# Gate matrices of a PEER layer: accumulated in DRAM by indirect transfers instead of one-hot matmuls

## The chip, the cores and the metric

The kernel runs on one core of a Trainium2 chip. The metric is the device time of one execution in microseconds (us); smaller is better. TensorE appears as PE (its weight loads as PEld), VectorE as DVE, ScalarE as ACT, GpSimd as POOL and SyncE as SP. Each of them executes its own list of instructions strictly in order.

## The reference

One layer of a residual block for 1024 tokens of width 1024, in float32. A mixer (mLSTM heads and gMLP groups, then an output projection) is followed by PEER, a layer of 16384 single-neuron experts. Per token and head (8 heads), two top-16 searches over 128 keys each give 256 candidate sums, of which the 16 best name 16 experts:

```python
s1, i1 = lax.top_k(s[:, :, 0], PEER_TOPK)
s2, i2 = lax.top_k(s[:, :, 1], PEER_TOPK)
cand = s1[..., :, None] + s2[..., None, :]          # reshaped to 256
cand_idx = i1[..., :, None] * PEER_KEYS + i2[..., None, :]
top_s, pos = lax.top_k(cand, PEER_TOPK)
idx = jnp.take_along_axis(cand_idx, pos, axis=-1)
gate = jax.nn.softmax(top_s, axis=-1)
...
a = jax.nn.gelu(jnp.einsum('td,thkd->thk', xb, ub))  # ub, vb: rows idx of expert_u, expert_v
out = jnp.einsum('thk,thkd->td', a * gb, vb)
```

So each token has 8 x 16 = 128 pairs of an expert (i, j), each index below 128, and a gate. Written as a matrix, the gates of a token are G[j, i], zero but for those pairs; where two heads of a token pick the same expert, their gates add up.

## The kernel before, in words

The tokens are eight blocks of 128. Blocks 0 to 4 are "dense": for them every expert is computed by matmul and multiplied with the gate matrix. Blocks 5 to 7 are "sparse": their experts' rows are gathered from DRAM by indirect transfers that POOL issues, and DVE does the dot products and sums.

**The front** goes over three parts, `PARTS = [(0, 2), (2, 3), (5, 3)]`: blocks 0 and 1, blocks 2 to 4, blocks 5 to 7. In each part come the normalisation (`scales`, ending in the reciprocal root `rx`), the mixer's steps (`head`, `group`), the output projection, a second normalisation (`rall`, one per block, made on POOL by `rstd` and needed by the transposes ahead of the queries), and the eight query heads, whose scores go to DRAM (`d_sc`). Between the query heads run the top-16 searches of the part's first block (`topk_units`; `merge16` does four heads at a time, so each block has two merges).

**Side work.** While part p+1 runs, the gate matrices of part p's dense blocks and the remaining top-16 searches are interleaved with it (`side_units`, `interleave`): blocks 0 and 1 beside part 1, blocks 2, 3 and 4 beside part 2. A gate matrix is made four tokens at a time (`gate_units`): DVE writes one-hots AB of both indices by comparing with `iota`, ACT scales one of them by the gates, PE multiplies them into PSUM tile pG (4 matmuls), ACT copies pG into Gt, and after 32 tokens ACT issues the store of Gt (2 MB) to `d_G`.

**The dense phase** (`experts`) has 32 groups of four expert rows i. Stage 1 reads the group's gates from `d_G` into tile Gin (one buffer), computes x times u (tile pa), gelu, times Gin (DVE), and splits the product into wh and wl. Stage 2 multiplies with v (tile pout) and DVE adds it to the accumulator. POOL makes the low halves ulo and vlo and issues the sparse blocks' gathers (768 of them, 128 rows of 4 KB each).

**What sets the order.** The program is written in the order above; a scheduler of the tile layer then fixes each engine's list at build time by its own estimates. On the chip nothing is moved any more: an instruction waits for its semaphores, and all behind it on its engine wait too. POOL's list holds the small steps of both normalisations and of the mixer (`rstd` at lines 62 and 63 of before, 61 and 62 of the change; the products `vv` at 409 and 410), so whatever stands ahead of them delays them.

Of the kernel before, what the change touches and what calls it, by code (L numbers as in the profile page):

```python
# [22 lines left out]
NEXP = 128  # L23
EPS = 1e-6
KAPPA = 0.25 * 128.0 ** -0.5
TG = 32
# [3 lines left out]
GS = 4  # L30
HB = 4
MMB = 2
TPB = 2
# [13 lines left out]
class Build:  # L47
# [124 lines left out]
    def consts(self, cp):  # L172
# [9 lines left out]
        self.rall = cp.tile([128, 8], F32, name="rall", tag="rall")  # L182
        self.mhalf = cp.tile([128, 16], F32, name="mhalf", tag="mhalf")
# [269 lines left out]
    def topk_units(self, blk):  # L453
# [15 lines left out]
        def merge(h0):  # L469
            ijg = st["ijg"]  # L470
            self.merge16(h0, st["tv"], st["ti"], ijg)
            if blk in self.sparse:
# [4 lines left out]
                hl = slice(h0 * 16, (h0 + HB) * 16)  # L477
                v.scalar_tensor_tensor(ix[:, hl], ijg[:, 0, hl], float(NEXP), ijg[:, 1, hl], op0=OP.mult, op1=OP.add)
                v.tensor_copy(gt[:, hl], ijg[:, 2, hl])

        def done():
            ijg = st["ijg"]
            if blk in self.dense:
                pt = self.gps.tile([128, 3, 128], F32, name="pG", tag="pG", bufs=2)
                for k in range(3):
                    nc.tensor.transpose(pt[:, k], ijg[:, k], self.ident)
                t = self.gp.tile([128, 3, 128], F32, name="ijgT", tag="ijgT", bufs=1)
                nc.scalar.activation(t, pt, AF.Copy)
                self.pick[blk] = t
# [5 lines left out]
        return L + [done]  # L495
# [145 lines left out]

    def gate_units(self, blk):
        nc = self.nc
        pool = self.gp
        s = self.dense.index(blk)
        st = {}

        def quad(tt, q):
            t3 = self.pick[blk]
            if q == 0:  # L650
                st["G"] = pool.tile([128, NEXP, TG], F32, name="Gt", tag="Gt", bufs=2)
            Gt = st["G"]
            pg = self.gps.tile([128, 4, 128], F32, name="pG", tag="pG", bufs=2)
            AB = pool.tile([128, 2, 4, 128], F32, name="AB", tag="AB", bufs=NAB)
            t0 = tt * TG + q * 4
# [7 lines left out]
            if q == TG // 4 - 1:  # L663
                nc.scalar.dma_start(self.d_G[s * (128 // TG) + tt], Gt)

        return [lambda tt=tt, q=q: quad(tt, q) for tt in range(128 // TG) for q in range(TG // 4)]

# [88 lines left out]
    def experts(self, side, dp, ps):  # L756
# [6 lines left out]
        T2 = T // 2  # L763
        n32 = T // TG
        ngroups = NEXP // GS
        W, V, st = {}, {}, {"n": 0}

        def stage1(g, e):
            if e == 0:
                st["G"] = dp.tile([128, n32, GS, TG], F32, name="Gin", tag="Gin", bufs=1)  # L770
                nc.sync.dma_start(st["G"], self.d_G[:, :, g * GS:(g + 1) * GS].rearrange("n j i t -> j n i t"))
# [10 lines left out]
            for s in range(2):  # L782
                pa = ps.tile([128, T2], F32, name="pa", tag="pa", bufs=3)
# [9 lines left out]
        def stage2(g):  # L793
# [9 lines left out]
            for s in range(ND):  # L803
                for d in range(2):
                    if st["n"] % 3 == 0:
                        po = ps.tile([128, 512], F32, name="pout", tag="pout", bufs=1)
                    else:
                        po = self.gps.tile([128, 512], F32, name="pout", tag="pG", bufs=2)
# [188 lines left out]
```

## Time and profile before

| | us |
|---|---|
| median of three runs | 2876.03 (2875.09 to 2885.14) |
| the profiled execution's own time | 2879.65 |
| span of that execution | 2877.8 |
| PE busy | 2708.7 (94%) |
| DVE busy | 2195.1 (76%) |
| POOL busy | 1501.2 (52%) |
| ACT busy | 1120.9 (39%) |

The span is the time from the first instruction to the last; the rest of the execution's time lies around it. The front lasts until about 992 us after the span's start, the dense phase from there to the end. POOL's busy time does not count register and semaphore instructions.

### The profile page before, as it was taken

The page shows a single profiled execution, that of the slowest core. Times are in us where ns is not written, and L with a number is a line of the kernel's source. Part 1 is how long each engine was busy: PE and PEld are TensorE (multiplying, and loading weights), DVE is VectorE, ACT ScalarE, POOL GpSimd, SP SyncE. Part 2 cuts the span into 40 slices and gives each one's busy share as a digit, 9 for nine tenths or more (in the row PEclk, how much of TensorE's full clock was granted, in tenths as well). Part 3 has the DMA queues.
Part 4 walks back from the last instruction along what each step waited for, and adds up shares of the span by engine and source line. Part 5 has one row for each costly group of instructions (what it writes and reads, how often), then busy time and mean ns, then how long its engine had stood idle before and what let it go on. Part 6 is the DMA issues. An engine that isn't in the chain of part 4 may idle for free.

```text
span 2877.8 us, 44768 instructions
## 1 busy us (share of the span) xinstructions
PE 2708.7 (94%) x16283; PEld 2470.3 (86%) x16283; DVE 2195.1 (76%) x4981; ACT 1120.9 (39%) x2295; POOL 1501.2 (52%) x1220
## 2 busy tenths in 40 slices
PE   7888989999898799999989999999999999999998
PEld 7887989889898798888878889889888899888987
DVE  6649975289985677888887787978987777777774
ACT  5444788348888332223222222223222232222222
POOL 3430010000100186777766677767767777768772
PEclk9989999999999899999999999999999999999999
DMA  7798557866578798998988999998889999989992
GB/s 245 256 313 281 188 211 280 276 223 225 187 272 302 264 326 300 323 336 306 333 288 304 336 321 331 308 342 308 309 280 331 344 327 332 334 314 332 326 345 95
DMA packets 327821, 838.41 MB, mean 291 GB/s; under 512 B 25520, under 2 KB 161072, under 8 KB 315824
## 3 DMA queue, kind: packets, MB, share of 16 engines
q0 software_dynamic: 114048, 427.87, 40.2%
q1 hardware_dynamic: 190544, 347.91, 37.5%
q10 hardware_dynamic: 23008, 59.77, 5.3%
q8 instruction: 128, 2.10, 0.3%
q14 instruction: 93, 0.76, 0.1%
HBM read 746.32 MB, written 89.13 MB: 290 GB/s over the span
## 4 chain that ended last, share of the span: by engine, by line
PE 58%; DVE 17%; DMA 9%; issue 6%; ACT 4%; POOL 4%; SPq 1%; ACTq 1%; POOLq 0%; DVEq 0%
PE pa L96 7%; PE pa L94 7%; PE pa L95 7%; PE pout L94 7%; PE pout L95 7%; PE pout L96 7%; DMA Gin<-d_G 3%; PE pG L661 3%; DVE sacc L713 2%; DVE gat L697 2%; PE pq L94 2%; PE pq L96 1%; PE pq L95 1%; DVE AB L656 1%; DMA raw<-v 1%
## 5 line engine op out<-in xcount | busy, mean ns | idle before, releaser
L94 PE MATMUL pa<-xh,uhi 128*128 128x320 f32 x2048 | 639.7, 312 | 42.2 <-DVE wl L790 26.4
L95 PE MATMUL pa<-xl,uhi 128*128 128x320 f32 x2048 | 637.3, 311 | 0.0
L96 PE MATMUL pa<-xh,ulo 128*128 128x320 f32 x2048 | 626.3, 312 | 4.2 <-POOL ulo L779 3.9
L94 PE MATMUL pout<-vhi,wh 128*128 128x512 f32 x1280 | 503.5, 398 | 17.4 <-DVE acc L814 15.4
L713 DVE SCALAR_TENSOR_TENSOR sacc<-gat,aw,sacc 128x1024 f32<-128x1024 f32 x384 | 492.3, 1282 | 30.6 <-DMA gat<-v,ix 22.8
L95 PE MATMUL pout<-vlo,wh 128*128 128x512 f32 x1280 | 507.4, 398 | 0.0
L709 POOL DMA_INDIRECT gat<-v,ix x384 | 364.3, 949 | 240.7 <-DVE sacc L713 140.0
L96 PE MATMUL pout<-vhi,wl 128*128 128x512 f32 x1280 | 488.5, 398 | 0.0
L693 POOL DMA_INDIRECT gat<-u,ix x384 | 365.5, 952 | 202.6 <-DVE gat L697 102.3
L697 DVE SCALAR_TENSOR_TENSOR gat<-gat,xn 128x1024 f32<-128x1024 f32 x384 | 459.5, 1212 | 15.3 <-DMA gat<-u,ix 15.1
L94 PEld LDWEIGHTS pa<-xh,uhi 128*128 128x128 f32 x2048 | 389.6, 190 | 56.1 <-DVE wl L790 30.7
L96 PEld LDWEIGHTS pa<-xh,ulo 128*128 128x128 f32 x2048 | 386.1, 190 | 11.1 <-POOL ulo L779 7.1
L95 PEld LDWEIGHTS pa<-xl,uhi 128*128 128x128 f32 x2048 | 389.6, 190 | 6.9
L779 POOL TENSOR_TENSOR ulo<-raw,uhi 128x1024 fp32r<-128x1024 f32 x128 | 309.0, 2416 | 144.0 <-ACT uhi L778 142.1
L800 ACT ACTIVATE vhi<-raw 128x1024 fp32r<-128x1024 f32 x128 | 131.8, 1052 | 504.4 <-PE pout L95 442.3
L801 POOL TENSOR_TENSOR vlo<-raw,vhi 128x1024 fp32r<-128x1024 f32 x128 | 307.9, 2416 | 34.1 <-ACT vhi L800 31.7
L94 PEld LDWEIGHTS pout<-vhi,wh 128*128 128x128 f32 x1280 | 241.7, 189 | 73.7 <-DVE acc L814 19.2
L814 DVE TENSOR_TENSOR acc<-acc,pout 128x512 f32<-128x512 f32 x320 | 214.5, 682 | 109.1 <-PE pout L96 96.0
L95 PEld LDWEIGHTS pout<-vlo,wh 128*128 128x128 f32 x1280 | 242.2, 189 | 50.6 <-POOL vlo L801 0.4
L96 PEld LDWEIGHTS pout<-vhi,wl 128*128 128x128 f32 x1280 | 240.2, 189 | 52.8
L788 DVE TENSOR_TENSOR pa<-pa,Gin 128x320 f32<-128x320 f32 x256 | 126.6, 494 | 202.2 <-ACT pa L786 108.0
L789 ACT ACTIVATE wh<-pa 128x320 fp32r<-128x320 f32 x256 | 111.8, 437 | 423.7 <-DVE pa L788 340.7
(243 smaller groups left out, 5039.4 us busy)
## 6 DMA issues: line engine op xcount, KB each, us to landing
raw<-uT SPq DMA_DIRECT2D x128, 512.0 KB
raw<-v SPq DMA_DIRECT2D x128, 512.0 KB
wlo<-d_wl SPq DMA_DIRECT2D x48, 1024.0 KB
d_G<-Gt ACTq DMA_DIRECT2D x20, 2048.0 KB
Gin<-d_G SPq DMA_DIRECT2D x32, 1280.0 KB
wraw<-win SPq DMA_DIRECT2D x72, 512.0 KB
d_wl<-wlo POOLq DMA_DIRECT2D x24, 1024.0 KB
wraw<-wq SPq DMA_DIRECT2D x48, 512.0 KB
```

The lines of the kernel that those rows point to most:

```text
L94: te.matmul(ps, lh, rh, start=k == 0, stop=False)
L95: te.matmul(ps, lh, rl, start=False, stop=False)
L96: te.matmul(ps, ll, rh, start=False, stop=k == n - 1)
L693: gd = nc.gpsimd.indirect_dma_start(out=t, out_offset=None, in_=self.I["u"], in_offset=bass.IndirectOffsetOnAxis(ap=st["ix"][:, k:k + 1], ...
L697: v.scalar_tensor_tensor(t, t, 1.0, st["xn"], op0=OP.mult, op1=OP.mult, accum_out=st["a"][:, k:k + 1])
L709: gd = nc.gpsimd.indirect_dma_start(out=t, out_offset=None, in_=self.I["v"], in_offset=bass.IndirectOffsetOnAxis(ap=st["ix"][:, k:k + 1], ...
L713: v.scalar_tensor_tensor(st["acc"], t, st["a"][:, k:k + 1], st["acc"], op0=OP.mult, op1=OP.add)
L779: nc.gpsimd.tensor_tensor(ul, ur, uh.bitcast(F32), op=OP.subtract)
L788: v.tensor_tensor(p3, p3, G[:, s * (n32 // 2):(s + 1) * (n32 // 2), e], op=OP.mult)
L800: nc.scalar.activation(vh, vr, AF.Copy)
L801: nc.gpsimd.tensor_tensor(vl, vr, vh.bitcast(F32), op=OP.subtract)
L814: v.tensor_add(st["acc"][:, s, dl], st["acc"][:, s, dl], po)
```

## The change

The gate matrices no longer come from one-hots and matmuls. There is now one DRAM tensor per dense block, laid out as [j, i, token]. SP stores zeros into it (4 transfers of 2 MB per block). Then POOL issues, for each of the 128 (head, rank) pairs of a block, one indirect transfer with accumulation: 128 single floats, one per token, each added at its own address. DVE computes the addresses (`dix`) from the indices and the token number (`pcol`). The transfers of one head (16 of them) may overlap; those of the next head of the same block wait until all 16 of the head before have landed, since two heads of a token may name the same expert. That makes 5 x 128 = 640 indirect transfers and 20 clearing stores; gone are the one-hots, their matmuls, the two PSUM banks of pG and the 20 stores of Gt. The two banks go to the front's tiles (3 buffers each in place of 2) and to pout. A group's gates are read by five transfers with rows of 2 KB instead of one with rows of 512 bytes, and stage 1 takes the 640 tokens in pieces of 256 and 384 in place of 320 and 320.

```diff
-MMB = 2
-TPB = 2
+MMB = 3
+TPB = 3
...
-        def done():
...
-                pt = self.gps.tile([128, 3, 128], F32, name="pG", tag="pG", bufs=2)
...
+                at = tk.tile([128, 16 * HB], F32, name="at", tag="at", bufs=1)
+                v.tensor_scalar(at, ijg[:, 0, hl], 128.0, self.pcol, op0=OP.mult, op1=OP.add)
+                v.scalar_tensor_tensor(ix[:, hl], ijg[:, 1, hl], 128.0 * NEXP, at, op0=OP.mult, op1=OP.add)
+            v.tensor_copy(gt[:, hl], ijg[:, 2, hl])
...
+    def clear_units(self, blk):
+
+        s = self.dense.index(blk)
+        self.cleared[blk] = []
+        flat = self.d_G[s].rearrange("j i t -> j (i t)")
+
+        def clear(q):
+            out = flat[:, q * 4096:(q + 1) * 4096].rearrange("j (a c) -> j a c", c=1024)
+            d = self.nc.sync.dma_start(out, self.zero[:, None, :].to_broadcast([128, 4, 1024]))
+            self.tc.keep_in_program_order(d)
+            self.cleared[blk].append(d.ins)
+
+        return [lambda q=q: clear(q) for q in range(4)]
+
     def gate_units(self, blk):
...
-            nc.vector.tensor_tensor(AB, self.iota[:, None, None, :].to_broadcast([128, 2, 4, 128]),
-                                    t3[:, 0:2, t0:t0 + 4, None].to_broadcast([128, 2, 4, 128]), op=OP.is_equal)
-            for u in range(4):
-                nc.scalar.activation(AB[:, 1, u], AB[:, 1, u], AF.Copy, scale=t3[:, 2, t0 + u:t0 + u + 1])
-            for u in range(4):
-                nc.tensor.matmul(pg[:, u], AB[:, 1, u], AB[:, 0, u], start=True, stop=True)
-            nc.scalar.activation(Gt[:, :, q * 4:q * 4 + 4], pg.rearrange("p q i -> p i q"), AF.Copy)
...
+        def some(h, q):
+            ix, gt = self.pick[blk]
+            key = f"G{blk}h{h}"
+            for k in range(h * 16 + q * 4, h * 16 + q * 4 + 4):
+                d = nc.gpsimd.indirect_dma_start(out=flat, out_offset=bass.IndirectOffsetOnAxis(ap=ix[:, k:k + 1], axis=0),
+                                                 in_=gt[:, k:k + 1], in_offset=None, compute_op=OP.add).ins
+                tc.declare_no_dep(d, group=key, reason="the experts of one head of a token differ, tokens differ")
+                tc.add_to_no_dep_group(key, d)
+                for e in st["before"]:
+                    tc.add_manual_dep(d, e.name, sync, reason="after the head before")
+                st["now"].append(d)
+            if q == 3:
+                st["before"], st["now"] = st["now"], []
+                self.filled[blk] = st["before"]
+
+        return [lambda h=h, q=q: some(h, q) for h in range(8) for q in range(4)]
...
-        T2 = T // 2
+        halves = [(0, ND // 2), (ND // 2, ND)]
...
-                nc.sync.dma_start(st["G"], self.d_G[:, :, g * GS:(g + 1) * GS].rearrange("n j i t -> j n i t"))
+                st["G"] = dp.tile([128, ND, GS, 128], F32, name="Gin", tag="Gin", bufs=1)
+                for b, blk in enumerate(self.dense):
+                    d = nc.sync.dma_start(st["G"][:, b], self.d_G[b][:, g * GS:(g + 1) * GS])
+                    for f in self.filled[blk]:
+                        self.tc.add_manual_dep(d.ins, f.name, sync, reason="after the last head")
...
+                    po = ps.tile([128, 512], F32, name="pout", tag="pout", bufs=3)
```

What this does to POOL's list is seen at two places. The first is the end of the mixer in part 1 (the norm `rall` of blocks 2 to 4 is what the queries of that part wait for; d_G_63 is the gate tensor of block 1, and x16 stands for 16 transfers in a row). Before:

```order
L63 TENSOR_TENSOR grr<-grr,mhalf 128x3
L409 TENSOR_TENSOR vv<-vv,lng 128x384
L410 TENSOR_TENSOR vv<-vv,lnb 128x384
L392 MEMSET ws 64x64
L62 TENSOR_SCALAR rall<-ss 128x1
```

Now:

```order
L62 TENSOR_TENSOR grr<-grr,mhalf 128x3
L672 DMA d_G_63<-dgt,dix 2097152x1 x15
L414 TENSOR_TENSOR vv<-vv,lng 128x384
L672 DMA d_G_63<-dgt,dix 2097152x1
L397 MEMSET ws 64x64
L415 TENSOR_TENSOR vv<-vv,lnb 128x384
L672 DMA d_G_63<-dgt,dix 2097152x1 x16
L397 MEMSET ws 64x64
L672 DMA d_G_63<-dgt,dix 2097152x1 x16
L61 TENSOR_SCALAR rall<-ss 128x1 x2
```

Where the steps of the mixer stood next to each other, transfers of block 1 now stand between them, and 32 more stand right ahead of `rall`. From the last store of part 0's weights to this `rall` POOL's list now holds 240 of the 640 transfers; 80 more stand from there to the first step of part 2's mixer (64 of these behind `rx`), 272 more up to `rall` of part 2.

The second place is the end of part 2 on the same engine, where the front gives way to the dense phase (d_G_66 is block 4; ulo is the dense phase's first step on POOL). Before:

```order
L62 TENSOR_SCALAR grr<-mv 128x3
L63 TENSOR_TENSOR grr<-grr,mhalf 128x3
L409 TENSOR_TENSOR vv<-vv,lng 128x384
L410 TENSOR_TENSOR vv<-vv,lnb 128x384
L62 TENSOR_SCALAR rall<-ss 128x1
L63 TENSOR_TENSOR rall<-rall,mhalf 128x1
...
L779 TENSOR_TENSOR ulo<-raw,uhi 128x1024 x2
```

Now:

```order
L415 TENSOR_TENSOR vv<-vv,lnb 128x384
L672 DMA d_G_66<-dgt,dix 2097152x1 x32
L61 TENSOR_SCALAR rall<-ss 128x1 x2
L62 TENSOR_TENSOR rall<-rall,mhalf 128x1 x2
L61 TENSOR_SCALAR rall<-ss 128x1
L62 TENSOR_TENSOR rall<-rall,mhalf 128x1
L672 DMA d_G_66<-dgt,dix 2097152x1 x48
L799 TENSOR_TENSOR ulo<-raw,uhi 128x1024 x2
```

Here 32 transfers of block 4 stand between the mixer's last product and `rall`, and the last 48 between `rall` and the first `ulo`.

## Rows read from the trace of the kernel before

Stretches are cut where POOL's list shows a part's border: 303 is the first POOL step of part 1's mixer, 485 its `rall`, 653 the first POOL step of part 2's mixer, 843 its `rall`, 992 the first `ulo` of the dense phase.

**Rows 1.** Busy time by stretch; us from the span's start, then per engine busy us.

```profile
core 0: us, PE busy (x) PEld busy (x) DVE busy (x) ACT busy (x) POOL busy (x), PEclk, DMA share, GB/s
0.00:229.00 229.00, 193.24 (x1397) 180.66 (x1398) 138.22 (x344) 107.62 (x201) 94.76 (x102) 0.91 0.84 277
229.00:303.00 74.00, 65.90 (x429) 56.49 (x429) 70.18 (x356) 39.85 (x68) 0.00 (x0) 0.98 0.71 245
303.00:485.00 182.00, 169.60 (x1313) 162.32 (x1312) 142.91 (x367) 152.22 (x412) 24.09 (x33) 0.96 0.59 213
485.00:653.00 168.00, 154.87 (x982) 143.25 (x981) 93.33 (x454) 78.87 (x153) 5.47 (x12) 0.97 0.78 269
653.00:843.00 190.00, 174.46 (x1330) 166.34 (x1329) 178.30 (x628) 159.62 (x418) 20.86 (x28) 0.97 0.58 209
843.00:992.00 149.00, 124.38 (x861) 122.73 (x860) 86.28 (x296) 95.93 (x244) 3.33 (x6) 0.94 0.81 283
992.00:2810.00 1818.00, 1769.88 (x9685) 1589.08 (x9686) 1452.90 (x2498) 468.03 (x770) 1332.98 (x1022) 0.99 0.92 322
```

**Rows 2.** Timeline of POOL: start, us, engine, line, idle before and its releaser.

```profile
303.06 0.18 POOL L62 TENSOR_SCALAR grr<-mv 128x3 f32<-128x3 f32 x1 [74.11 <-DVE mv L404]
...
484.97 0.19 POOL L62 TENSOR_SCALAR rall<-ss 128x1 f32<-128x1 f32 x1 [46.77 <-DVE ss L143]
...
653.29 0.11 POOL L313 MEMSET va<- 128x3 f32 x1 [121.74 <-PE pn L351]
...
843.65 0.19 POOL L62 TENSOR_SCALAR rall<-ss 128x1 f32<-128x1 f32 x1 [58.20 <-DVE ss L143]
...
992.00 4.96 POOL L779 TENSOR_TENSOR ulo<-raw,uhi 128x1024 fp32r<-128x1024 f32 x2 [139.15 <-ACT uhi L778]
```

**Rows 3.** Instructions of line 693: ns min/median/max, first and last start.

```profile
L693 POOL DMA_INDIRECT gat<-u,ix x384: 932/941/1479, 997.1 to 2513.1; - x192
```

**Rows 4.** Timeline of POOL at the first gathers of the dense phase.

```profile
997.13 1.48 POOL L693 DMA_INDIRECT gat<-u,ix  x1 [0.17 <-DVE cu L524]
...
1000.17 1.31 POOL L693 DMA_INDIRECT gat<-u,ix  x1 [0.30 <-issue]
...
1041.49 0.94 POOL L693 DMA_INDIRECT gat<-u,ix  x1 [0.30 <-issue]
1042.73 0.94 POOL L693 DMA_INDIRECT gat<-u,ix  x1 [0.30 <-issue]
```

**Rows 5.** Instructions of line 83, the plain store issued by POOL.

```profile
L83 POOL DMA_DIRECT2D d_wl<-wlo x24: 571/601/782, 22.0 to 228.4; - x24
```

**Rows 6.** Timeline of DVE, where a first half of a top-16 ends.

```profile
242.57 0.22 DVE L544 TENSOR_TENSOR ijg<-cs,gsum 128x64 f32<-128x64 f32 x1
...
586.51 0.20 DVE L544 TENSOR_TENSOR ijg<-cs,gsum 128x64 f32<-128x64 f32 x1
```

**Rows 7.** Waits in the stretch 300 to 1000: total us, times, longest.

```profile
DVE tv L549 <- DMA scb<-d_sc: 49.1, 15, 9.4
```

**Rows 8.** The chain that ended last, in order of time: start, us, what.

```profile
2610.55 7.03 DMA gat<-v,ix
...
2791.19 19.57 DMA Gin<-d_G
```

**Rows 9.** Groups by line and shape: busy us, mean ns, idle before and releaser.

```profile
L659 ACT ACTIVATE AB<-AB,ijgT 128x128 f32<-128x128 f32 x640 | 203.0, 396 | 36.5 <-DVE AB L656 25.0 <-DMA xh<-d_xh 10.3 <-DVE s L553 0.4
...
L656 DVE TENSOR_TENSOR AB<-iota,ijgT 128x1024 f32<-128x1024 f32 x160 | 195.7, 1229 | 59.6 <-PE pG L661 48.2 <-ACT sc L446 5.7 <-ACT whi L77 1.6
L661 PE MATMUL pG<-AB 128*128 128x128 f32 x1280 | 184.3, 285 | 19.8 <-ACT Gt L662 10.2 <-ACT AB L659 9.5
...
L662 ACT ACTIVATE Gt<-pG 128x512 f32<-128x512 f32 x160 | 93.0, 588 | 27.0 <-PE pG L661 26.2
```

**Rows 10.** Busy time of the instructions on tile pG, last stretch of the front.

```profile
843.00:992.00 149.00, 42.15 (x307) 40.03 (x306) 22.41 (x39) 0.94 0.81 283
```

**Rows 11.** Waits from 992 to the end: total us, times, longest.

```profile
DVE pa L788 <- DMA Gin<-d_G: 55.9, 10, 9.5
```

More of the change, by code (lines that the diff above doesn't have):

```diff
@@ L25 @@
 KAPPA = 0.25 * 128.0 ** -0.5
-TG = 32
 DENSE = [0, 1, 2, 3, 4]
@@ L476, in merge @@
                 ix, gt = self.pick[blk]
-                hl = slice(h0 * 16, (h0 + HB) * 16)
                 v.scalar_tensor_tensor(ix[:, hl], ijg[:, 0, hl], float(NEXP), ijg[:, 1, hl], op0=OP.mult, op1=OP.add)
-                v.tensor_copy(gt[:, hl], ijg[:, 2, hl])
-        def done():
-            ijg = st["ijg"]
-            if blk in self.dense:
-                pt = self.gps.tile([128, 3, 128], F32, name="pG", tag="pG", bufs=2)
[L485 to L489, printed above, removed]
+            else:
+                if h0 == 0:
+                    self.pick[blk] = (self.kp.tile([128, 128], I32, name="dix", tag="dix", bufs=3),
+                                      self.kp.tile([128, 128], F32, name="dgt", tag="dgt", bufs=3))
+                ix, gt = self.pick[blk]
[3 more added lines that the diff above has]
+            v.tensor_copy(gt[:, hl], ijg[:, 2, hl])
         L = []
@@ L666, in gate_units @@
-        return [lambda tt=tt, q=q: quad(tt, q) for tt in range(128 // TG) for q in range(TG // 4)]
+        flat = self.d_G[s].rearrange("j i (t o) -> (j i t) o", o=1)
+        st = {"before": self.cleared[blk], "now": []}
+        sync = mybir.DependencyInfo(mybir.DependencyClass.Sync, mybir.DependencyReason.DATA)
+        def some(h, q):
+            ix, gt = self.pick[blk]
+            key = f"G{blk}h{h}"
[10 more added lines that the diff above has]
+                self.filled[blk] = st["before"]
@@ L781, in stage1 @@
             wl = dp.tile([128, T], F32R, name="wl", tag="wl", bufs=GS + 1)
-            for s in range(2):
-                pa = ps.tile([128, T2], F32, name="pa", tag="pa", bufs=3)
-                sl = slice(s * T2, (s + 1) * T2)
+            for b0, b1 in halves:
+                w = (b1 - b0) * 128
+                pa = ps.tile([128, w], F32, name="pa", tag="pa", bufs=3)
+                sl = slice(b0 * 128, b1 * 128)
                 self.mm3(pa, [((uh[:, c], ul[:, c]), (xh[:, c, sl], xl[:, c, sl])) for c in range(8)])
                 nc.scalar.activation(pa, pa, AF.Gelu_apprx_tanh)
-                p3 = pa.rearrange("p (n t) -> p n t", t=TG)
-                v.tensor_tensor(p3, p3, G[:, s * (n32 // 2):(s + 1) * (n32 // 2), e], op=OP.mult)
+                p3 = pa.rearrange("p (n t) -> p n t", t=128)
+                v.tensor_tensor(p3, p3, G[:, b0:b1, e], op=OP.mult)
                 nc.scalar.activation(wh[:, sl], pa, AF.Copy)
@@ L887, in run @@
             self.d_wl = scratch("d_wl", [24, 128, 8, 256])
-            self.d_G = scratch("d_G", [ND * 128 // TG, 128, NEXP, TG])
+            self.d_G = [scratch(f"d_G{s}", [128, NEXP, 128]) for s in range(ND)]
             cp = ctx.enter_context(tc.tile_pool(name="const", bufs=1))
@@ L894, in run @@
             self.tk = ctx.enter_context(tc.tile_pool(name="topk", **right))
+            self.gp = ctx.enter_context(tc.tile_pool(name="gates", **right))
             self.consts(cp)
[L896 to L897 removed]
             self.tkb = 1
```

37 lines of the change are left out of this document (13 added, 24 removed).

## The prediction

> **What bounds the kernel now.** I read the busy time by stretch first [rows 1]. PE is busy for 1770 of the 1818 us of the dense phase, and for 92 to 93% of the mixer stretches (303 to 485, 653 to 843): PE is the bound nearly everywhere. POOL is the opposite: in the front from 229 to 992 it is busy for 0.0 + 24.1 + 5.5 + 20.9 + 3.3 = 54 us of 763. The POOL timeline [rows 2] shows that it sits waiting for DVE, PE or ACT, up to 139 us at a time. So a kernel bound by PE is to give up PE, ACT and DVE work in the front, and to put 640 transfers on an engine that looks free there. What decides is whether 640 transfers fit into some 700 free microseconds, and what stands behind them on POOL.
>
> **What is removed.** The one-hots, their scaling, matmuls and copies were 195.7 us of DVE, 203.0 + 93.0 of ACT and 184.3 of PE [rows 9], all in the front. That is a gain only where those engines still set the pace; below, POOL sets it in both mixer stretches, so there I count nothing. The two added buffers of the front's PSUM tiles go the same way. In the last stretch POOL has little in front of PE, so there it counts: pG held PE for 42 of 124 busy us [rows 10, 1]. I take 25 of the 42, since matmuls overlap and the weights' loads go on, and keep 0 and 42 as ends.
>
> **The price of one add, P.** No accumulating transfer and no scatter is in the trace. The nearest row is the gather: also indirect, also 128 descriptors, 932/941/1479 ns min/median/max [rows 3]. In a row, gathers start 1.24 us apart, 0.94 busy plus 0.30 in between [rows 4]. Those issued while DVE was in the top-16 took 1.48 and 1.31 instead of 0.94 [rows 4], and the adds run beside five blocks' top-16. So P = 1.30 us, a little above the gather in a row. Lower end: the plain store's 0.60 [rows 5] plus the 0.30, 0.90 us. Upper end: if reading the destination doubles the descriptors' work, 2 x 0.94 = 1.88 us.
>
> The Trainium skill, "DMA: Bandwidth & Descriptors", section "Anatomy of one DMA — SWDGE (gpsimd) path", puts a fixed cost of about 2.0 us on every DMA that GpSimd issues; taken as the spacing of the adds it would make the sum below about 3613 us. The gathers' starts 1.24 us apart speak against that reading: what is fixed is latency, and it overlaps from one transfer to the next.
>
> **The price of a head's border.** The next head of the same block waits until the last of the 16 has landed. A small load that DVE waits for costs it 49.1 / 15 = 3.3 us [rows 7]; a gather of 512 KB on the chain takes 7.0 [rows 8]. I take 3 us where nothing of another block stands between: POOL's list has 8 such borders up to `rall` of part 1, 3 in the next stretch, 4 in the one after (three more are hidden at the end). With 7 us, the 15 would cost 60 more.
>
> **The path.** POOL works in order, `rall` is what the query's transposes wait for, and `rx` what the next part waits for. So I follow POOL's list, with the counts that it gives:
>
> - Start. The first half of block 0's top-16 ends at 243 [rows 6]; `dix` follows. The 8 MB of zeros are new DMA work beside part 0's weights: 8.4 MB at that stretch's 277 GB/s are 30 us, and with 16% of the DMA engines' time free there [rows 1] I add half, 15: 258.
> - Part 1 up to `rall`: 240 adds x 1.30 = 312, 8 borders x 3 = 24, POOL's own steps there 24 [rows 1], 10 for waits on DVE and PE: 258 + 370 = 628. Before, 485 [rows 2]: 143 late.
> - `rall` to part 2's mixer. The 64 adds of block 2 need its first top-16 half, which came 586.5 - 485.0 = 101 us after `rall` [rows 6, 2], at PE's pace of the queries, with no gate work there to remove. Then 64 x 1.30 + 3 x 3 = 92. (The 16 adds ahead of `rx`, 21 us, fit inside the 101.) 628 + 193 = 821. Before, 653.
> - Part 2 up to `rall`: 272 x 1.30 = 354, 4 x 3 = 12, own steps 21 [rows 1], 25 for waits, more than in part 1 because 32 adds (42 us) cover less of the output projection that ends the mixer (58 us idle on POOL before [rows 2]): 412. 1233. Before, 843: 390 late.
> - `rall` to the first `ulo`: 149 before, less the 25 of pG, 124. The last 48 adds, 62 us and three borders, are over before that. 1357. Before, 992.
> - Dense phase and end. 2878 - 992 = 1886 before. PE idles 48 us in it [rows 1]; DVE waits 55.9 us in all, 10 times, for Gin [rows 11], and the chain holds a Gin load of 19.6 us [rows 8], though 1.28 MB at that stretch's 322 GB/s would take 4. The load now has a quarter as many rows, four times as long, so it should get through the gathers' traffic faster: I take 35 of the 56 as gained. Ends: nothing, and 56. Five loads in place of one cost SP four more issues a group, under 2 us of 57; 256 and 384 columns are 640 as before. 1851.
>
> 1357 + 1851 = 3208. The profiled execution took 2879.65 for a span of 2877.8, so 2 us more: **3210 us**, 11.6% above the median of 2876.03 (the profiled execution itself lies 0.1% above that median). POOL has 576 adds on this path, so each 0.1 us of P moves the time by 58 us: 608 + 576 P is the start of the dense phase.
>
> **Rivals.**
>
> *Faster: cheap adds.* If an add costs POOL little, POOL's gaps swallow them and the front loses 184 us of PE and 296 of ACT. The point from which this decides is where 608 + 576 P + 1851 equals 2878: P = 0.73 us. At the plain store's bare 0.60 [rows 5] the time would be 608 + 346 + 1851 + 2 = 2807. For it: one float per descriptor in place of 4 KB. Against it: the store, whose addresses need no table, and whose rows are twice as long as a gather's, already takes 0.60 without the 0.30 gap, and the gather 0.94; the work goes with descriptors and indices, not with bytes. Chance 0.06.
>
> *No change.* P between 0.71 and 0.75, which would need the gap of 0.30 to vanish too: within 14 us of 2876. Chance 0.02.
>
> *Much slower: the DMA engines become the bound.* POOL's list has a transfer wait for the one eight ahead of it, so at most eight are under way. If a landing takes over 8 x 1.30 = 10.4 us, landings set the pace. Each of 16 DMA engines gets 8 floats a transfer, to be read in DRAM, added and written; one after the other at 2 us each that is 16 us, P = 2.0, and the 15 borders cost 13 more each: 3210 + 0.70 x 576 + 195 = 3808. For it: the front's DMA is 58 to 81% busy already [rows 1], and no landing of this kind is in the trace. Against it: a gather that moves a thousand times the bytes lands in 7.0 us [rows 8]. Chance 0.13.
>
> Against that serial reading stands the Trainium skill too, "DMA: Bandwidth & Descriptors", section "Two DMAs through the same engine are not ordered": a read-modify-write packet that directly followed another one of the same bytes on one engine mostly read stale data, so an engine has several under way at once. No run here shows it yet.
>
> **How the numbers follow.** The forecast, POOL's queue as the front's bound with P from 0.90 to 1.88, has 0.79, and spans 2979 to 3544 us; the loose ends of the dense phase (35 down, 21 up), of pG (25 and 17) and of the borders (60) lie inside. The predicted time is its middle case, 3210. The range of 8 in 10 is that span rounded, 2980 to 3550: it leaves out the cheap adds and most of the DMA-bound case, 2 in 10. A measurement of this kernel can tell about 0.5%, 14 us. Faster by more than that 0.06, within it 0.02, slower 0.92.
>
> **What would show it.** In the changed kernel's profile, POOL's indirect adds should have a mean near 1.0 us and start about 1.3 apart, with idle time before the first of a head put down to the DMA; POOL's busy share from 260 to the first `ulo` should be 60% or more where it was 7%; the first `ulo` should start near 1357 (front wrong if under 1250 or over 1500), `rall` of the two parts near 628 and 1233. PE should be idle for hundreds of microseconds in the front, waiting for DVE, ACT and POOL steps of the mixer, and the granted clock lower there. From the first `ulo` to the end should take about 1850 us, with less than 20 us of DVE waits for Gin. The prediction is wrong in its mechanism if POOL idles in the mixer stretches while the end still comes late, or if the first `ulo` comes before 992.

## The result: slower by a fifth, and the profile after

The changed kernel takes 3477.99 us (median of 4 runs, 3476.35 to 3486.19); the kernel before took 2875.56 on the same chip. That is **1.2098 times as long, with an interval of 1.2058 to 1.2138**. The forecast was 3210, the range 2980 to 3550. The profiled execution took 3478.32 for a span of 3476.6.

Busy time by stretch, changed kernel (us of the stretch, then busy us and number of instructions of each engine). The stretches are cut where POOL's list shows the same borders as before: `rall` of part 1 at 755, the first POOL step of part 2's mixer at 996, `rall` of part 2 at 1530, the first `ulo` at 1644.

```profile
core 0: us, PE busy (x) PEld busy (x) DVE busy (x) ACT busy (x) POOL busy (x), PEclk, DMA share, GB/s
0.00:243.00 243.00, 187.88 (x1389) 174.39 (x1390) 136.58 (x352) 104.97 (x199) 94.78 (x101) 0.92 0.86 295
243.00:755.00 512.00, 199.00 (x1295) 177.45 (x1295) 142.11 (x671) 92.51 (x180) 396.89 (x274) 0.69 0.54 134
755.00:996.00 241.00, 162.01 (x1003) 151.41 (x1003) 100.85 (x528) 78.44 (x142) 134.69 (x92) 0.83 0.75 224
996.00:1530.00 534.00, 122.40 (x790) 110.64 (x790) 99.89 (x509) 49.76 (x103) 442.58 (x302) 0.59 0.35 53
1530.00:1644.00 114.00, 89.13 (x529) 88.16 (x529) 44.36 (x259) 33.10 (x56) 76.59 (x54) 0.87 0.81 224
1644.00:3476.00 1832.00, 1799.35 (x9984) 1618.35 (x9984) 1490.89 (x2538) 484.93 (x803) 1351.16 (x1040) 0.99 0.89 322
```

Before, PE was busy for 92 to 93% of the mixer stretches and POOL for 11 to 13% [rows 1]. Now it is the other way round: from 996 to 1530 POOL has 443 us of work in 534, and PE 122. The dense phase became shorter, 1832.6 us to the end against 2877.8 - 992.0 = 1885.8. So the front lost 1644.0 - 992.0 = 652 us, and the dense phase gave 53 back.

The adds, by their source line (ns min/median/max, first and last start; then what POOL's idle time before them ended with, us and times):

```profile
L672 POOL DMA_INDIRECT d_G<-dgt,dix x640: 1533/1545/3493, 264.6 to 1628.4; - x160
...
  issue: 187.9, 622
  DMA d_sc<-sc: 47.5, 1
  DMA d_G<-dgt,dix: 42.9, 11
  DVE dix L492: 20.7, 1
```

The chain that ended last by engine, and the adds as a group, on the page of the changed kernel (busy us, mean ns | idle before):

```profile
PE 50%; POOL 26%; DVE 9%; issue 7%; DMA 4%; ACTq 2%; ACT 1%; SPq 1%; POOLq 0%; DVEq 0%
...
L672 POOL DMA_INDIRECT d_G<-dgt,dix x640 | 1007.7, 1574 | 300.0 <-issue 187.9
```

And their landing, from the view of the DMA issues (median us):

```profile
d_G<-dgt,dix POOLq DMA_INDIRECT x640, 3.0
```

An add keeps POOL busy for 1.574 us in the mean, where a gather takes 0.941 [rows 3]; the gap between two of them is 187.9 / 640 = 0.294, as between gathers [rows 4]. So P = 1.868 us, and 640 of them are 1195 us.

Waits in the front, 264 to 1530 (us in total, times, longest):

```profile
PE pm L417 <- POOL vv L415: 403.8, 6, 114.2
ACT ah L110 <- PE tp L105: 403.5, 8, 91.0
DVE nat L420 <- PE pm L417: 378.4, 7, 88.8
...
DVE hrr L381 <- POOL hrr L62: 176.4, 5, 78.2
```

PE's matmul `pm` waits for a product on POOL (line 415), up to 114 us at a time, behind the adds in POOL's list. DVE and ACT then stand behind PE. From 264 to 1644 POOL has 1050 us of work and 188 us of issue gaps in 1380; its other waits come to 159, 21 of them ahead of the first add.

### The profile page after: what moved, and what is told of

It reads as the page before. It is cut to its first block, busy times and chain, and to the rows that moved or that the text cites. A ratio compares the mean times of both kernels' runs of the same rounds, so it can differ in the third digit from the quotient of the medians.

```text
span 3476.6 us, 41972 instructions
## 1 busy us (share of the span) xinstructions
PE 2559.8 (74%) x14988; PEld 2320.4 (67%) x14988; DVE 2014.7 (58%) x4854; ACT 843.7 (24%) x1482; POOL 2496.7 (72%) x1860
## 4 chain that ended last, share of the span: by engine, by line
PE 50%; POOL 26%; DVE 9%; issue 7%; DMA 4%; ACTq 2%; ACT 1%; SPq 1%; POOLq 0%; DVEq 0%
POOL d_G L672 24%; PE pout L93 8%; PE pout L95 8%; PE pout L94 8%; PE pa L95 7%; PE pa L93 7%; PE pa L94 7%; DMA d_G<-dgt,dix 1%; PE pq L93 1%; DVE gat L714 1%; PE pq L95 1%; PE pq L94 1%; ACTq L628 1%; DVE sacc L730 1%; ACTq L629 1%
## 5 line engine op out<-in xcount | busy, mean ns | idle before, releaser
L672 POOL DMA_INDIRECT d_G<-dgt,dix x640 | 1007.7, 1574 | 300.0 <-issue 187.9
L93 PE MATMUL pa<-xh,uhi 128*128 128x256 f32 (+1 forms) x2048 | 633.1, 309 | 27.1 <-ACT uhi L798 15.2
L94 PE MATMUL pa<-xl,uhi 128*128 128x256 f32 (+1 forms) x2048 | 631.5, 309 | 0.0
L95 PE MATMUL pa<-xh,ulo 128*128 128x256 f32 (+1 forms) x2048 | 621.4, 309 | 3.1 <-POOL ulo L799 3.1
L95 PE MATMUL pout<-vhi,wl 128*128 128x512 f32 x1280 | 490.4, 396 | 0.7 <-DVE wl L811 0.7
L417 PE MATMUL pm<-vv,ws 128*128 128x384 f32 (+1 forms) x24 | 14.9, 715 | 416.2 <-POOL vv L415 404.7
```

Source lines behind the costliest of these rows:

```text
L93: te.matmul(ps, lh, rh, start=k == 0, stop=False)
L94: te.matmul(ps, lh, rl, start=False, stop=False)
L95: te.matmul(ps, ll, rh, start=False, stop=k == n - 1)
L672: d = nc.gpsimd.indirect_dma_start(out=flat, out_offset=bass.IndirectOffsetOnAxis(ap=ix[:, k:k + 1], axis=0), in_=gt[:, k:k + 1], in_offse ...
```

## The experiments

On the chip of the first four runs the kernel before took 2889.58 us (one run), on that of the next four 2887.36, on that of the last two 2890.93; on the chip of the result it was 2875.56. So times from different chips differ by up to 0.5% for the same kernel. The small kernel and the next three runs were each made once, and their times have no interval. Each stage below is read from the run's own profile.

### What POOL pays for, measured alone (price)

A small kernel that computes nothing of the layer: rows of indirect transfers, nothing else on DVE at the time. The row that matters, and its two variants:

```diff
+ indirect_dma_start(out=f_put,  out_offset=off(fx, k),     in_=junk[:, k:k + 1],    in_offset=None)
+ indirect_dma_start(out=f_add,  out_offset=off(fx, k),     in_=junk[:, k:k + 1],    in_offset=None, compute_op=OP.add)
+ indirect_dma_start(out=f_half, out_offset=off(fx, k, 64), in_=junk[0:64, k:k + 1], in_offset=None, compute_op=OP.add)
```

> This kernel computes nothing of the layer: it issues rows of indirect transfers from POOL on an otherwise idle chip, 128 addresses each unless said: 16 gathers of 4 KB rows, 32 gathers of single floats, 32 plain scatters of single floats, 32 scatters of single floats with accumulation, 32 of those with 64 addresses, 16 scatters of 4 KB rows with accumulation. Theory A, the accumulation itself makes each descriptor dearer for POOL: 0.94 us for both gathers and for the plain scatter, 1.54 for both accumulating ones, whatever the bytes, and with 64 addresses clearly under 1.2. Rival B, an indexed destination (or a row of 4 bytes) is dear: the plain scatter takes 1.54 too (or the gather of floats does). Rival C, DVE's work beside it made the adds slow: here, with DVE idle, they take 0.94.

POOL's groups of that kernel (busy us, mean ns | idle before): in this order the accumulating scatter of a float, the same with 64 addresses, the plain scatter, the gather of a float, the accumulating scatter and the gather of a row of 4 KB.

```profile
L112 POOL DMA_INDIRECT d_add<-junk,fx x32 | 49.5, 1546 | 9.8 <-issue 9.8
L116 POOL DMA_INDIRECT d_half<-junk,fx x32 | 45.5, 1422 | 9.8 <-issue 9.8
L109 POOL DMA_INDIRECT d_put<-junk,fx x32 | 30.7, 959 | 9.8 <-issue 9.8
L106 POOL DMA_INDIRECT one<-x,sx x32 | 30.2, 943 | 20.7 <-DMA big<-u,rx 13.3 <-issue 7.0 <-DMA one<-x,sx 0.3
L120 POOL DMA_INDIRECT d_row<-big,rx x16 | 24.8, 1551 | 4.9 <-issue 4.9
L103 POOL DMA_INDIRECT big<-u,rx x16 | 15.2, 951 | 16.3 <-DMA big<-u,rx 9.9 <-DVE sx L80 3.9 <-issue 2.5
```

The scatter itself costs what the gather does (0.959 against 0.943). The accumulation adds 0.587 us of POOL's time, with an idle DVE and no other traffic, and a row a thousand times longer adds next to nothing (1.551 against 1.546). One expectation missed: with half the addresses the instruction was to come clearly under 1.2 us, and it took 1.422, only 0.124 less. By these two points, on a straight line, 128 addresses are an estimated 0.25 us of the 1.55, and 1.3 go with the instruction.

### No adds at all (no_adds)

The gate matrices stay zero: the 640 adds are left out, everything else of the change stays.

```diff
-        return [lambda h=h, q=q: some(h, q) for h in range(8) for q in range(4)]
+        self.filled[blk] = self.cleared[blk]
+        return []
```

> The changed kernel without its 640 adds: the gate matrices stay zero, so the dense blocks' expert sums are left out of the result; the clears, the dense phase and all else stay. Theory A, POOL's queue of adds is all that keeps the front long, and the freed PE, ACT and DVE time is real but hidden behind it: the front ends earlier than before the change (992 us), by some 100 us, the first dense step at 860 to 920, and with a dense phase of 1837 the time is 2700 to 2760. Rival E, the clearing stores, the new buffers or the order cost something too: first dense step at 992 or later, time 2830 or more.

Measured: 2697.6 us, 2 us under theory A's range, with the first `ulo` inside it. POOL's timeline at the first `ulo` (start, us; idle before):

```profile
871.23 2.37 POOL L800 TENSOR_TENSOR ulo<-raw,uhi 128x1024 fp32r<-128x1024 f32 x1 [109.21 <-ACT uhi L799]
```

The front ends at 871 where it ended at 992. So the work that the change removes, with the buffers that it adds, was worth 121 us of front when nothing takes its place. The prediction gave it 25, because it expected POOL to cover the rest. The 640 adds then cost 1644 - 871 = 773 us of front.

### The adds without accumulating (plain_scatter)

The scatters only write: an expert picked by two heads of a token keeps one gate in place of the sum. POOL's list is the same, instruction for instruction.

```diff
-   in_=gt[:, k:k + 1], in_offset=None, compute_op=OP.add).ins
+   in_=gt[:, k:k + 1], in_offset=None).ins
```

> The changed kernel with the accumulation taken out of the 640 scatters: each writes its float instead of adding it, so that gates of an expert picked by two heads of a token are not summed. Nothing else differs. Theory A: an add's 1.57 us becomes 0.95, and with 576 of them on POOL's path the first dense step comes 576 x 0.62 = 357 us earlier, the time is 3478 - 357 = 3121 (3060 to 3180). Rival B: no change of POOL's 1.57, time 3478 within 20. Rival D, landings of the read-modify-writes set the pace and not POOL: the scatter's POOL time stays under 1.0 but the time falls by less than 100.

Measured: 3368.35 us. The price fell as the small kernel says, which refutes rival B, but the front moved by 115 us only and the time by 110: not theory A's 357, and nearly rival D's "less than 100". The scatters by source line:

```profile
L672 POOL DMA_INDIRECT d_G<-dgt,dix x640: 952/958/1532, 271.2 to 1456.6; - x160
```

POOL's timeline at the first `ulo`:

```profile
1528.56 4.75 POOL L799 TENSOR_TENSOR ulo<-raw,uhi 128x1024 fp32r<-128x1024 f32 x2 [70.95 <-ACT uhi L798]
```

And POOL's waits from 264 to 1530 (us in total, times, longest):

```profile
POOL d_G L672 <- issue: 190.9, 626, 2.0
POOL ulo L799 <- ACT uhi L798: 71.0, 1, 71.0
POOL d_G L672 <- DMA d_sc<-sc: 47.3, 1, 47.3
POOL rall L61 <- DVE ss L142: 45.5, 6, 27.0
POOL rx L61 <- DVE ss L142: 44.6, 3, 41.3
POOL va L318 <- PE pu L364: 43.1, 2, 33.8
POOL va L318 <- PE pn L356: 41.9, 1, 41.9
```

POOL's sum shrank by 383 us (640 x (1.868 - 0.971 - 0.298)), and 261 of them came back as waits of POOL, for DVE, PE and ACT: without the issue gaps they are 420 us in all, 159 in the changed kernel. POOL takes its list in order: at each of the mixer's steps in it, POOL waits for the mixer if the mixer is late, and the mixer waits for POOL if the adds are. Two explanations of that were left: waits in turns on POOL's ordered list (theory L below), and transfers that hold the front (rival T).

The run has something else that no other run shows. Between instructions of the mixer PE sits idle without any releaser that the profile names, 383 us in 206 gaps from 264 to 1530; in every other run of the layer such gaps come to 1.4 us at most. Two of them, 109 us, end as POOL's `vv` ends, so they are waits for POOL. The others lie mostly between matmuls of one product, 1 to 3 us each (PE's waits; us in total, times, longest):

```profile
PE pm L417 <- issue: 109.4, 2, 57.2
...
PE pg L93 <- issue: 43.1, 20, 21.2
```

What caused these gaps is not shown, and the run was made once. They delay the mixer whatever stands on POOL, so the 115 us are not the measure of theory L alone.

### The small steps moved off POOL (steps_off_pool, put_steps_off)

The mixer's products, its small memsets and the norms' power function leave POOL, so that from the first add on its list holds the adds and the dense phase's work alone. The power function becomes a logarithm and an exponential on ACT.

```diff
-        g = self.nc.gpsimd
+        g = self.nc.vector
...
-        g.tensor_tensor(dst, dst, self.mhalf[:, :n], op=OP.pow)
+        self.nc.scalar.activation(dst, dst, AF.Ln)
+        self.nc.scalar.activation(dst, dst, AF.Exp, scale=-0.5)
...
-        nc.gpsimd.tensor_tensor(vv, vv, gr[0][:, None, :].to_broadcast([128, self.nb, 128]), op=OP.mult)
+        nc.vector.tensor_tensor(vv, vv, gr[0][:, None, :].to_broadcast([128, self.nb, 128]), op=OP.mult)
```

First with the accumulating adds:

> The changed kernel with all of the mixer's and norms' small steps taken off POOL: the two products on vv and the memsets on DVE, the reciprocal root as Ln and Exp on ACT. Only the adds (and part 0's weights) stay on POOL in the front. Theory A1, POOL's sum of adds sets the end of the front, wherever they stand: 264 + 640 x 1.88 plus about 45 of borders, and some 65 of the dense phase's own POOL steps that now stand between the last adds, so Gin is complete near 1580 and the time is 3400 (3340 to 3440). Rival A2, the harm is that the mixer's steps queue behind the adds: with them gone PE runs through the front as before, and the time falls below 3100.

Measured: 3400.41 us. The adds, and the mixer's last step `nat` on DVE, by source line:

```profile
L672 POOL DMA_INDIRECT d_G<-dgt,dix x640: 1541/1542/3332, 279.6 to 1568.0; - x160
```
```profile
L420 DVE SCALAR_TENSOR_TENSOR nat<-pm,bs,gu x12: 474/602/618, 81.6 to 839.6; 128x384 f32<-128x384 f32 x8, 128x256 f32<-128x256 f32 x4
```

The mixer is through at 840, where it ended at 1464 in the changed kernel. The time falls by 78 us only, since the dense phase needs all gates and POOL is busy with the adds until 1570; a product `pa` of the dense phase waits for them until 1574:

```profile
DVE pa L809 <- DMA Gin<-d_G: 58.7, 1, 58.7
```

This is theory A1: the sum of the adds alone nearly fills the front, wherever the mixer's steps stand.

Then with the plain scatter on top (same left-out sum as above):

> The two earlier edits together: the scatters lose their accumulation (values of the gate matrices are then wrong) and the mixer's and the norms' small steps leave POOL for DVE and ACT. It is to tell why the plain scatter alone, at 1.26 us per instruction where the accumulating one took 1.87, moved the start of the dense phase by 115 us only and not by 640 x 0.61 = 390. Theory L (order on POOL): with the mixer's steps inside POOL's in-order list, POOL and the mixer wait for one another in turns, and a cheaper scatter turns into waits; with the steps elsewhere the mixer ends near 840 us as in the run with the steps off POOL, POOL's list is the sum alone, and the dense phase starts near 280 + 640 x 1.26 + 60 = 1145 us; with 1835 for the rest the time is near 2980 (2940 to 3050). Rival T (transfers): the scatters' landings or the gathers hold the front whatever stands on POOL, so that the dense phase still starts near 1530 and the time stays above 3250.

Measured: 3049.48 us (ratio 1.0555, 1.0516 to 1.0595). The scatters by source line, and POOL's waits from 264 to 1224:

```profile
L672 POOL DMA_INDIRECT d_G<-dgt,dix x640: 952/958/2867, 281.9 to 1222.5; - x160
```
```profile
POOL d_G L672 <- issue: 189.6, 622, 0.5
POOL d_G L672 <- DMA d_G<-dgt,dix: 36.8, 12, 7.3
```

This is what theory L expects: with the steps elsewhere, the cheaper scatter pays nearly in full. The last scatter starts at 1223 in place of 1568, 345 us earlier, and the time falls by 351 us of the 383; with the steps on POOL it fell by 110. PE's gaps of the run before are not here, so they do not come with the plain scatter as such. The time is at the upper end of what was expected; 51 us of POOL's work among the scatters are the dense phase's first gathers and casts (24 and 9 instructions), which that number left out. Rival T is refuted: transfers do not hold the front, borders cost 37 us in all.

### Half of the adds (half_heads)

Only the adds of heads 0 to 3 are issued, still accumulating; the gates of the other heads are left out.

```diff
+            if h >= 4:
+                return
...
-            if q == 3:
+            if q == 3 and h < 4:
```

> The changed kernel with the adds of heads 0 to 3 alone: 320 adds in place of 640, each still accumulating (half of the gates are left out of the sum). Theory L (waits in turns): what POOL loses in adds comes back in part as waits between the mixer's steps in POOL's list, as with the plain scatter; the dense phase starts between 1200 and 1350 us, the time is 3040 to 3190. Rival S (POOL's sum alone sets the front, as the prediction's formula has it): the start moves by 320 x 1.87 = 598 us, to about 1046, and the time is near 2880.

Measured: 3086.33 us (ratio 1.0683, 1.0643 to 1.0723). POOL's timeline at the first `ulo`, and its longest waits from 264 to 1247:

```profile
1246.94 2.37 POOL L801 TENSOR_TENSOR ulo<-raw,uhi 128x1024 fp32r<-128x1024 f32 x1 [109.09 <-DMA raw<-uT]
```
```profile
POOL ulo L801 <- DMA raw<-uT: 109.1, 1, 109.1
POOL d_G L674 <- issue: 91.2, 301, 0.7
POOL d_G L674 <- DVE dix L492: 72.4, 2, 51.5
POOL rx L61 <- DVE ss L142: 54.4, 3, 51.0
POOL rall L61 <- DVE ss L142: 52.3, 5, 42.0
```

This lies in theory L's ranges, and rival S is refuted: POOL has 1195 - 600 = 595 us less of adds, and the front moves by 397. POOL's waits without the issue gaps are 356 us, 159 in the changed kernel; PE has none of the plain scatter's gaps here. Put together, the front's end against the POOL time of the adds from the start at 264 (count by mean and gap):

| run | adds on POOL, us | first `ulo`, us | front that the adds do not fill, us |
|---|---|---|---|
| no adds | 0 | 871 | 607 |
| half of the heads | 320 x (1.590 + 0.285) = 600 | 1247 | 383 |
| plain scatter | 640 x (0.971 + 0.298) = 812 | 1529 | 452 |
| the change | 640 x 1.868 = 1195 | 1644 | 185 |

The last column is the mixer's time that is not hidden behind adds. It doesn't fall to nothing as soon as the adds fill POOL's old gaps. The plain scatter's row lies above that of the half although its scatters take longer; its gaps on PE are in it, and a straight line between the half and the change would put 812 us of adds at an estimated 1388 in place of 1529. So the column doesn't show whether the sum alone decides; the next run shows that the place of the adds counts too.

### The dense phase's gate tile (short_rows, before_long_rows, before_five_loads)

The change also altered how the dense phase loads its gate tile: five transfers with rows of 2 KB in place of one with rows of 512 bytes. DVE's waits for the tile fell from 55.9 us [rows 11] to 0.4, and the phase became 53 us shorter. DVE's wait in the changed kernel:

```profile
DVE pa L809 <- DMA Gin<-d_G: 0.4, 1, 0.4
```

Which difference did it? First the changed kernel with rows of 512 bytes again (the layout's line; the addresses, the clears, the loads and the product's view follow it):

```diff
-scratch(f"d_G{s}", [128, NEXP, 128])
+scratch(f"d_G{s}", [128 // TG, 128, NEXP, TG])
...
```

> The changed kernel with the gate matrices laid out as before, in rows of 32 tokens: a gate tile then comes in 512-byte pieces and not in 2 KB pieces; adds, their number and their order stay. Theory R (row length): DVE waits for the gate tiles again, 40 to 56 us in the dense phase, which goes from 1837 back to 1875 to 1890 us; the time is 3515 to 3530, 1.222 to 1.228 times the kernel before. Rival N (the five separate loads or the product's other tile shape made the dense phase shorter): it stays at 1837, the time at 3478, 1.21 times the kernel before.

Measured: 3454.78 us (ratio 1.1956, 1.1920 to 1.1992). The waits did not come back: no row of DVE's product `pa` waiting for the tile, and from the first `ulo` at 1622.3 to the end at 3452.8 it takes 1830.5 us. Theory R is refuted for the changed kernel. The 22 us by which the front became shorter were in no theory. They are there by `rall` of part 1, which starts at 731.8 in place of 755.0, and stay to the end. POOL's list has 16 adds less ahead of it (POOL on the gate tensors up to `rall`: us, busy us and number, clock, DMA share, GB/s; the changed kernel, then this run):

```profile
200.00:754.90 554.90, 378.57 (x240) 0.71 0.57 149
```
```profile
200.00:731.70 531.70, 351.93 (x224) 0.72 0.60 161
```

The 16 adds stand behind that `rall` instead, where the changed kernel's POOL waits 47.5 us for the first addresses of block 2 (the profile names `d_sc`, but `dix` ends 0.3 us before the add starts) and this run's 19.5. There they lengthen nothing: the two runs take 241 and 242 us from `rall` to part 2's mixer. So the same adds cost less where POOL has to wait anyway.

Then the kernel before with long rows and no other edit (the store of Gt follows the layout), which answers the question from the other side:

```diff
-scratch("d_G", [ND * 128 // TG, 128, NEXP, TG])
+scratch("d_G", [128, NEXP // GS, ND * 128 // TG, GS * TG])
...
-nc.sync.dma_start(st["G"], self.d_G[:, :, g * GS:(g + 1) * GS].rearrange("n j i t -> j n i t"))
+nc.sync.dma_start(st["G"].rearrange("j n e t -> j n (e t)"), self.d_G[:, g])
...
```

> The kernel before with one edit: the gate matrices laid out so that a dense group's tile is one contiguous row of 10 KB per partition (the stores then write 512-byte pieces). No adds. Theory R: DVE's waits of 55.9 us for the gate tiles go, and the dense phase takes about 1837 us instead of 1886; the time is 2820 to 2840, 0.981 to 0.988 of the kernel before. Rival N (the waits were the place in the queue or the traffic, not the length of the pieces): within 10 us of the kernel before, or slower by the stores' smaller pieces.

Measured: 2838.76 us, **0.9825 of the kernel before (0.9802 to 0.9848)**. DVE's waits for the tile, kernel before with long rows:

```profile
DVE pa L788 <- DMA Gin<-d_G: 2.6, 2, 2.3
```

So longer pieces do end the waits, though short pieces need not cause them. What is left is the splitting, tried alone in the kernel before:

```diff
-nc.sync.dma_start(st["G"], self.d_G[:, :, g * GS:(g + 1) * GS].rearrange("n j i t -> j n i t"))
+for b in range(ND):
+    bl = slice(b * (128 // TG), (b + 1) * (128 // TG))
+    nc.sync.dma_start(st["G"][:, bl], self.d_G[bl, :, g * GS:(g + 1) * GS].rearrange("n j i t -> j n i t"))
```

> The kernel before with one edit: a dense group's gate tile is loaded by five transfers, one for each block of tokens, in place of one; the 512-byte pieces, the stores and the gates' making stay. It is to tell which of the two differences ended DVE's waits of 55.9 us for that tile, the longer pieces or the splitting, as the short rows kept the waits away in the changed kernel. Theory Q (one large transfer of short pieces is what is late; split, it comes in time): the waits fall under 10 us and the time is 2825 to 2850, 0.979 to 0.988 of the kernel before. Rival R (pieces of 512 bytes are late whichever way, and the changed kernel's dense phase escaped by another tile shape): the waits stay at 40 to 70 us and the time within 10 us of the kernel before.

Measured: 2841.08 us, 0.9847 of the kernel before (0.9814 to 0.9880). DVE's waits for the tile, kernel before with five loads, and the landing on its page (KB each, median us):

```profile
DVE pa L790 <- DMA Gin<-d_G: 5.4, 5, 2.5
```
```profile
Gin<-d_G SPq DMA_DIRECT2D x160, 256.0 KB, 8.4
...
DMA to landing us min/median/max: 3.0/8.4/18.6
```

Theory Q: DVE waits only with the combination of one large transfer and 512-byte pieces. Either cure alone nearly ends the waits. With long rows the one transfer of 1280 KB lands in 9.2 us in the median (the page of that run), where one of short pieces stood on the chain for 19.6 [rows 8]. Of the five loads one still takes 18.6 us, so short pieces can land late after splitting too; why DVE hardly waits for them is not shown. In both runs the dense phase takes 1846 us (from 997.7 and 993.7 to the end), 40 less than in the kernel before. The other 13 us of the changed kernel's 53 no run explains; its stage 1 in pieces of 256 and 384 tokens was not tried alone.

### A try to improve the front as well (long_rows_steps_off)

The kernel before with long rows, and the small steps moved off POOL by the edit above.

> The kernel before with the long rows, and with the mixer's and the norms' small steps moved from POOL to DVE and ACT. Theory A (the front of the kernel before waits for POOL's steps, which take 1.0 to 1.5 us each there, in a chain of products and norms): the dense phase starts 15 to 50 us earlier and the time is 2790 to 2825, 0.966 to 0.978 of the kernel before. Rival B (in the front the gates' one-hot work on DVE and PE is the bound, and DVE has the steps on top): 2835 to 2860, not better than the long rows alone at 0.9825.

Measured: 2942.83 us (ratio 1.0198, 1.0166 to 1.0231): theory A is refuted, and the loss is larger than rival B's. ACT's groups from 243 to 998 (busy us, mean ns) have rows that the kernel with long rows alone lacks or has fewer of:

```profile
L62 ACT ACT_TABLE_LOAD x24 | 30.8, 1283 | 2.7 <-issue 2.3
L63 ACT ACT_TABLE_LOAD x23 | 29.5, 1283 | 0.4
L402 ACT ACT_TABLE_LOAD x18 | 23.1, 1283 | 0.6 <-ACT kw L349 0.3
```

Lines 62 and 63 are the logarithm and the exponential. Nearly each of them loads a function table, and so do many of the users behind them: 65 loads of 1.283 us in these three groups, 83 us, on the engine that also scales the one-hots for PE; with long rows alone line 402 loads ten times for 12.8 us, the other two lines never. The dense phase started at 1092 in place of 998, 94 us later. That the 70 us of new loads are the larger part of this is how I read it; the products alone were not moved. The Trainium skill, "ScalarE: Activation LUTs", section "Table sets: the hidden batching unit", counts one load for a logarithm with an exponential behind it, since one set holds both; in this run 46 of 48 logarithms and 44 of 48 exponentials had a load of their own. Which sets were loaded the trace does not tell. The two runs with the steps off POOL above have these loads too, beside a front that the adds hold for longer, as the mixer's end at 840 shows.

The best versions measured are the kernel before with the gate rows made long, at 2838.76 us, and with five loads, at 2841.08; their intervals overlap.

## Why the prediction was right, and where it was off

**The mechanism held.** POOL, idle for nine tenths of the front, became its bound; in both mixer stretches it is the busiest engine, the mixer's steps wait for it, PE idles for hundreds of microseconds, and the granted clock of the two mixer stretches fell to 0.69 and 0.59 from 0.96 and 0.97 [rows 1], means of the levels 2.4 and 1.2 GHz over stretches in which PE was busy for 39 and 23% of the time. Undone alone (no adds), the front comes back and more; with the steps elsewhere the sum on POOL alone holds the end, 78 us below the change. By the prediction's own signs the size of the front was wrong: the first `ulo` came at 1644, over the 1500 that it had named, and `rall` of the two parts at 755 and 1530 in place of 628 and 1233.

**The price of an add was the first step that failed in size.** The prediction took 1.30 us, nearest to gathers in a row, and kept 1.88 as the upper end, "if reading the destination doubles the descriptors' work". Measured are 1.868. The number landed on that end by luck. The end leaves out the gap of 0.30 us that the lower end and the 1.30 count; with it, doubling gives 2.18 us and a time of 3717. And the reason was another: POOL's busy time rose by 0.587 us and not to the double, hardly with the addresses and not with the bytes. In the prediction's own sum the term is 576 x 0.568 = 327 us, more than the whole miss of 268.

**The rest, stretch by stretch,** with each add repriced at 1.868 (predicted length, repriced length, measured):

| stretch | predicted | repriced | measured |
|---|---|---|---|
| start, to the first add | 258 | 258 | 264.6 |
| to `rall` of part 1 | 370 | 506 | 490.4 |
| to part 2's mixer | 193 | 229 | 241.2 |
| to `rall` of part 2 | 412 | 566 | 533.5 |
| to the first `ulo` | 124 | 124 | 114.2 |
| to the end | 1851 | 1851 | 1832.6 |

Repriced, the sum is 3534 and the measured span 3476.6. What is left are small things. In the two mixer stretches the prediction had allowed 10 and 25 us for waits on DVE and PE; in the trace POOL waits 6.6 and 0.5 us for DVE there, and for PE not at all. That is most of the 33 us by which the second came out shorter. Borders: 15 at 3 us were 45; up to `rall` of part 2 33.9 us were measured, in 9 waits, at a landing of 3.0.

**The straight line was the second.** The prediction wrote the start of the dense phase as 608 + 576 P. Near the measured price, where POOL rarely waits, it is 40 us off: 608 + 576 x 1.868 = 1684 against 1644. For less work on POOL it falls too steeply. Its waits on DVE and PE were fixed numbers, taken as if the mixer would be ready whenever POOL reached one of its steps; with half of the adds 595 us less on POOL gave 397 us of front. At the plain scatter's 1.269 the line gives 1339, and the run shows 1529, though with its gaps on PE. How far the forecast's own premise, 1.30, was off is open between two values: the plain scatter's run would put the dense phase near 1529 and the time near 3370, a straight line between the half of the adds and the change (832 us of adds) near an estimated 1402 and 3240. So of the 287 us by which the first `ulo` came after 1357, the price is some 110 to 240, and the rest are waits that the sum did not let grow.

**The dense phase.** 35 of the 56 us of waits for the gate tile were counted as gained, for longer rows; 55.5 are gone. The stated cause was one of two: five loads with the short rows end nearly all of them too.

**The rivals.** Cheap adds needed 0.73 us, and even a scatter that adds nothing takes 0.96 + 0.30. The DMA-bound case needed landings over 10.4 us; the median is 3.0 and the longest, 9.3, stays under it too. The Trainium skill, "DMA: Bandwidth & Descriptors", section "Anatomy of one DMA — SWDGE (gpsimd) path", with its fixed cost of about 2.0 us per DMA from GpSimd, would as a spacing have made an estimated 3613, nearer to the measured 3478 than 3210 was. The small kernel shows starts 1.85 us apart for accumulating scatters and 1.26 for plain ones on the same engine, so no one fixed figure covers both.

## What to carry to other kernels

An engine that idles while it waits for others in an ordered list has free time to give only where it has to wait: there 16 adds lengthened nothing, while those put ahead of a step that is due delay every engine that waits for it. Less work there partly comes back as waits. Before hundreds of small indirect transfers replace matrix work, multiply their number by what the issuing engine pays for each, here 1.85 us for an accumulating one with 4 bytes or 4 KB per address, and compare that with the stage's length. Where a load of many short pieces is late, lengthen the pieces in DRAM or split the load: here either was worth 1.5 to 1.8% of the kernel.

## What the runs showed of the hardware that was not expected

- Accumulating costs the issuing engine: 1.546 us of POOL per indirect transfer against 0.959 for the plain scatter. Halving the addresses to 64 saves 0.124 us of it; rows of 4 KB in place of 4 bytes cost 0.005 more.
- The accumulating transfer of single floats lands early all the same: 3.0 us in the median, where the gathers of 4 KB rows of the same run take 6.8 and 6.2.
- One transfer of 1280 KB in 512-byte pieces made DVE wait for 55.9 us in all; five of 256 KB in the same pieces 5.4; one in 10 KB pieces 2.6.
- A logarithm and an exponential in turns on ACT, as built here, load a table nearly every time (90 of 96), 1.283 us each.
